# A decoder trunk's head in a new order, and the attention's two heads normalised on one engine

## The chip, the cores and the metric

The kernel runs on one core of a Trainium2 chip. The core has a matrix engine (TensorE, PE in the profile; its weight loads are listed as PEld), VectorE (DVE), ScalarE (ACT), GpSimd (POOL) and SyncE (SP), which here issues nearly all DMAs. Each engine takes its own instructions in their order; between engines they are ordered by semaphores. SBUF is the on-chip memory, PSUM the banks that PE accumulates in.

The metric is device time in microseconds (us) of one execution, as the median of several timed runs. A profiled execution is one more run, with a trace; its span reaches from the program's first instruction to its last.

## The reference

One layer of a decoder trunk, in float32, for a sequence of 2048 rows and a width of 1024:

```python
mod = jax.nn.silu(c) @ w_ada[l] + b_ada[l]
shift, scale, gate = jnp.split(mod, 3, axis=-1)
u = x * (1.0 + scale[:, None, :]) + shift[:, None, :]
h = u @ w_in[l]
q, k, v, a_gate, p_in, p_gate, m_a, m_p = jnp.split(h, offsets, axis=-1)
a = sliding_window_sink_attention(q, k, v, sinks[l], bias, mask) * jax.nn.silu(a_gate)
a = a @ w_attn_proj[l]
p = jnp.einsum('bsgc,gcd->bsgd', multiscale_causal_pool(p_in), w_pool_mix[l]).reshape(B, S, POOL_WIDTH)
p = (p * pool_scale[l]) * jax.nn.silu(p_gate)
p = p @ w_pool_proj[l]
y = jax.nn.sigmoid(m_a) * a + jax.nn.sigmoid(m_p) * p
y = (y @ w_out[l]) * (1.0 + gate[:, None, :])
x = layer_norm(DEEPNORM_ALPHA * x + y, ln_gain[l], ln_bias[l])
```

The attention has 16 query heads of 64 on 2 key heads, a window of 128 keys, a relative bias and one sink a head in the softmax. Before all of this, `mod` has to be known: a product of a 1024 vector with a 1024 x 3072 matrix.

## The kernel before

**Products.** The large products are made by a 2 x 2 block scheme with seven block products instead of eight. The activations of a chunk (two halves of 512 columns, eight tiles of 128 rows) are kept as seven sets in SBUF, `B11, T1, T2, B21, T3, B22, T4`: the blocks and their differences. A set has four tiles, and each tile a high and a low half in a reduced float format; a float32 product is three matmuls (`mm3`: high x high, high x low, low x high). Making a tile is a cast on ACT (the high half) and a subtraction on DVE (the low half): `parts`, `split_set`. The weights go the same way: a `Quad` (line 235) is a pair of 128 x 1024 weight tiles, loaded by `load_w` and `load_last`; `mid` (258) and `late` (268) are the differences of its blocks, and `split_part` (418) or `pair_split` makes high and low halves of two at a time (`w_set`). A quad's four stages are F (`B11, T1`), S (`T2, B21`), Th (`T3, B22`) and L (`T4`). It accumulates in three PSUM banks `a, b, c`; `behind` (451) evacuates and adds between the products, and `consume` takes each finished block.

**The order.** `plan` lists all products of all phases; `run` (477) walks through them. At a product's position it makes the weights' halves that are due, then issues the twelve matmuls, then `behind`, then `tick` (330): it runs the functions hung on that position (`at`, `hooks`) and those put off by `defer(ticks, f)` (313). So the place of a call in this walk is its place in the engine's queue, SP's too.

**The head** (`head`, 1212) comes before the walk. It computes `mod` tile by tile (k = 0 to 7), turns `x` into `u`, fills the first sets and makes the first group's products of stages F and S by itself, written out by hand. The group is two quads, `grp[0]` (keys and values) and `grp[1]` (queries 0 and 1). For each k: `opening(k)` is 16 one-column matmuls for `shift` (`pe_modulation`, 1256) and on DVE a multiply-reduce over 1024 columns for `scale` and an addition that waits for PE (`modulation`, 1263). `difference(k)` (1292, k < 4) subtracts the halves of `x`; `closing(k)` (1297) makes a tile of T1 from it (k < 4) or of T2 (k >= 4); `modulate_x(k)` applies scale and shift on ACT; `middle(k)` (1285) makes the tile of B11 (k < 4) or B21, and for k >= 4 first updates `ts[k - 4]`, from which T2 is made. `products(i)` (1312) issues tile i of B11 and T1 for both quads, `more(x, i)` (1339) tile i of T2 and B21 for quad x, six matmuls. `second_pair(x)` (1330) makes the weights of stage S and copies the accumulators `a` and `b` to a bank and a buffer, on ACT. `t3_sum(i)` (1307) makes the blocks of T3. `idle_products` are matmuls on a constant tile whose result is not used.

In the loop at line 1357, `closing` comes one or two turns after its `difference`, and the sets T3 and the third weights come after the last product. The head then returns four functions that the walk runs at its positions 0, 3, 4 and 5 (`late` of the second quad, the sets B22 and T4). The walk finds F and S of the first group done (`opened`) and begins with their `behind`.

Beside the first group run `fold_parts` (1108), which multiplies the pooling weights with the mixing matrix, and `gate_modulation`; both load through SP.

**The overlay** (`overlay`, 767) is the attention. Its 64 steps a chunk (two heads each) are spread between the matmuls of the phases `o0` and `o1`. `step(n)` (871) issues on PE: scores of n into the bank `lg`, transposes of n-2 into the bank `pt`, values of n-3 into `pv`. Both `lg` and `pt` are single banks. Then, for n-1, DVE takes the reciprocal of the softmax sums and the two heads are scaled: the first by ACT, the second by DVE's `tensor_scalar`. Then ACT casts `pt` to `pth` and copies a part of `pv`; for n, DVE reads `lg` for each head (a custom operation that adds the bias and takes the minimum) and ACT takes exponentials; then DVE subtracts `ptl` from `pt` and `pth`, which frees `pt`, and adds the outputs.

**Stores of q.** `q_quad` (574) scales a finished block on ACT, splits it on DVE and stores both halves two ticks later, from a ring of buffers `c`.

Of the kernel before, what the change touches and what calls it, by code (L numbers as in the profile page):

```python
# [59 lines left out]
def kernel(  # L60
# [174 lines left out]
    class Quad:  # L235
        def __init__(self, srcs, consume, sums=None, again=False):
            self.srcs, self.consume, self.sums, self.again = srcs, consume, sums, again
            self.at, self.parts, self.rings, self.opened, self.prefetch = {}, {}, {}, False, None

# [211 lines left out]
    def behind(ph, q, kind, h):  # L451
# [11 lines left out]
        elif kind == "S":  # L463
            if h == 0:
                dve.tensor_tensor(q.b, q.c, q.p5, ALU.add)
            else:
                q.consume(ph, 0, 0, q.a)
        elif kind == "Th":
            if h == 0:
                dve.tensor_tensor(q.p5, q.c, q.p5, ALU.add)  # L470
                q.consume(ph, 1, 1, q.p5)
            else:
                q.consume(ph, 0, 1, q.b)
        else:
            q.consume(ph, 1, 0, q.c)
# [98 lines left out]
    def q_quad(s, m):  # L574
        def consume(ph, mi, t, src):
            hi, lo = ph.c("q_hi", F32R), ph.c("q_lo", F32R)
            act.activation(hi, src, AF.Copy, scale=-0.125)
            dve.scalar_tensor_tensor(lo, src, -0.125, as32(hi), ALU.mult, ALU.subtract)
            defer(2, lambda: [sp.dma_start(q_d[s, m + mi, t, n], as32(x)) for n, x in enumerate((hi, lo))])
# [187 lines left out]
    def overlay(ph, s, n_slots):  # L767
# [103 lines left out]
        def step(n):  # L871
# [4 lines left out]
            if n - 1 in Es:  # L876
                E, e0, sm = Es.pop(n - 1)
                dve.reciprocal(sm, sm)
                act.activation(E[:, 0, e0:256], E[:, 0, e0:256], AF.Copy, scale=sm[:, 0:1])
                dve.tensor_scalar(E[:, 1, e0:256], E[:, 1, e0:256], sm[:, 1:2], None, ALU.mult)  # L880
# [331 lines left out]
    def head(ph, grp):  # L1212
# [50 lines left out]
        def modulation(k):  # L1263
            m = KT + k
            w = ws[k][1]
            dve.tensor_tensor_reduce(w, w, cb, 1.0, mod[:, m : m + 1], ALU.mult, ALU.add, mod[:, m : m + 1])
            dve.tensor_tensor(mod[:, k : k + 1], mod[:, k : k + 1], sums[k][:, 0:1], ALU.add)
# [13 lines left out]
        def opening(k):  # L1281
            pe_modulation(k)
            modulation(k)
# [63 lines left out]
        difference(0)  # L1347
        modulate_x(0)
# [3 lines left out]
        difference(1)  # L1352
        middle(0)
        closing(0)
        modulate_x(1)
        first_pair(1)
        for k in range(2, KT):
            if k == 6:
                second_pair(0)
                closing(4)  # L1360
            opening(k)
            if k < 4:
                difference(k)
            if 2 < k < 6:
                closing(k - 2)
            middle(k - 1)
            if k == 7:
                closing(5)
            modulate_x(k)
            if k < 6:  # L1370
                products(k - 2)
            if k < 4:
                grp[k - 2].mid(dve)
            if k == 6:
                more(0, 0)
                second_pair(1)
        more(1, 0)
        for x in range(2):
            more(x, 1)
        closing(6)  # L1380
        middle(7)
        closing(7)
        for i in range(2):
            t3_sum(i)
        for i in (2, 3):
            for x in range(2):
                more(x, i)
        grp[0].late(dve)
        for i in (2, 3):
            t3_sum(i)  # L1390
        sets["T3"] = set_tile("T3")
        for i in range(4):
            parts("T3", i, xs[i][0])
# [3 lines left out]
        grp[0].parts["Th"] = third  # L1397

# [10 lines left out]
        rest = (0, lambda: grp[1].late(dve)), (3, late_parts("B22", 1)), (4, t4_sums), (5, late_parts("T4", 0))  # L1409
        for q, o in zip(grp, opened):  # L1410
            q.a, q.b, q.c, _, q.p5 = o
            q.opened = True
        return rest
# [153 lines left out]
```

## Time and profile before

| | us |
|---|---|
| timed runs, median of 3 (lowest, highest) | 1715.49 (1715.05, 1715.85) |
| profiled execution, its own time | 1721.38 |
| its span | 1719.3 |
| mean granted clock of PE | 0.989 |
| busy: PE | 1672.1 |
| busy: DVE | 1274.5 |
| busy: ACT | 945.4 |
| busy: POOL | 590.5 |

Stretches of the profiled execution, in us from the span's start: the head up to about 65, the first phase of the walk to about 167, the overlays from about 168 to 490 and from 750 to 1075.

A row of a timeline reads: start, duration, engine, line, operation, what it writes `<-` what it reads by the program's names, shapes, how many in a row; in brackets the idle time of the engine before it and what ended it. The line is 56 for nearly all, that of a helper that records every operation, so rows are told apart by their names. A row "SPq" is a DMA being issued. A row of a chain of waits has start, duration, what.

### The profile page before, as it was taken

Reading aid. Unit: us, or ns where it says so; the run is one execution under the profiler, and the core shown is the slowest. Engines: PE = TensorE matmul, PEld = TensorE weight load, DVE = VectorE, ACT = ScalarE, POOL = GpSimd, SP = SyncE. Lnnn points to the kernel's source line nnn. Section 1 sums busy time; section 2 is a strip of 40 time slices with the busy share of each in tenths; the row PEclk is TensorE's granted clock in tenths of the full one; section 3 lists DMA queues with packets and bytes.
Section 4 is the critical chain, followed back from the end, with each engine's and each line's share of the span. In section 5 each row is a group of like instructions: output and inputs, shape, how many; then the busy total and the mean of one; then the engine's idle time right before and its main releaser. Section 6 shows DMA issues by size and latency. Waiting matters only on the chain.

```text
span 1719.3 us, 24847 instructions
## 1 busy us (share of the span) xinstructions
PE 1672.1 (97%) x8112; PEld 1400.3 (81%) x8112; DVE 1274.5 (74%) x2295; ACT 945.4 (55%) x1815; POOL 590.5 (34%) x563
## 2 busy tenths in 40 slices
PE   9899999989999999999999999999999999999997
PEld 7678788878788888888888888888878888888886
DVE  5956787778756778658877888487886785778778
ACT  3644687767753436447777676433454443434552
POOL 3012455545553223323334243322243311113544
PEclk8999999999999999999999999999999999999999
DMA  9389666766547789873555544489978695778343
GB/s 355 120 285 301 204 213 228 244 214 201 190 162 228 254 281 316 285 249 119 183 178 188 180 145 154 160 268 325 336 260 290 199 331 182 259 261 295 147 147 122
DMA packets 236545, 389.50 MB, mean 227 GB/s; under 512 B 20840, under 2 KB 90240, under 8 KB 236288
## 3 DMA queue, kind: packets, MB, share of 16 engines
q1 hardware_dynamic: 235344, 386.55, 66.9%
q10 hardware_dynamic: 1040, 1.34, 0.3%
q8 instruction: 64, 1.05, 0.3%
q14 instruction: 65, 0.53, 0.1%
q0 software_dynamic: 32, 0.02, 0.0%
HBM read 243.63 MB, written 147.35 MB: 227 GB/s over the span
## 4 chain that ended last, share of the span: by engine, by line
PE 74%; DVE 10%; DMA 6%; ACT 5%; issue 4%; SPq 1%; POOL 0%; DVEq 0%; ACTq 0%; POOLq 0%
PE mm L56 46%; PE lg L56 12%; PE c L56 10%; PE pv L56 3%; PE pt L56 3%; DVE w_set L56 3%; DVE L L56 2%; ACT L L56 2%; ACT w_set L56 1%; DVE wide L56 1%; SPq L56 1%; DMA A<-in_win_dram 1%; ACT sig L56 1%; DMA qs<-q_d 1%; ACT q_hi L56 1%
## 5 line engine op out<-in xcount | busy, mean ns | idle before, releaser
L56 PE MATMUL mm<-set_B,w_set 128*128 128x512 f32 x2664 | 655.6, 393 | 1.5 <-DVE w_set L56 1.3
L56 PEld LDWEIGHTS mm<-set_B,w_set 128*128 128x128 f32 x2664 | 498.5, 189 | 105.5 <-DVE w_set L56 2.2
L56 PE MATMUL mm<-set_T,w_set 128*128 128x512 f32 x1896 | 470.4, 395 | 1.7 <-DVE set_T L56 0.9
L56 POOL TENSOR_TENSOR W<-W 128x512 f32<-128x512 f32 x185 | 267.2, 1454 | 568.3 <-DVE w_set L56 373.7
L56 PEld LDWEIGHTS mm<-set_T,w_set 128*128 128x128 f32 x1896 | 354.9, 191 | 75.4 <-DVE set_T L56 1.6
L56 DVE TENSOR_TENSOR w_set<-W,w_set 128x1024 fp32r<-128x1024 f32 x197 | 254.7, 1293 | 111.9 <-ACT w_set L56 101.9
L56 ACT CAST w_set<-W 128x1024 fp32r<-128x1024 f32 x222 | 232.2, 1047 | 92.8 <-PE mm L56 52.9
L56 ACT ACTIVATE L<-L 128x257 f32<-128x257 f32 (+3 forms) x384 | 191.2, 500 | 117.8 <-DVE L L56 117.2
L56 PE MATMUL lg<-set_T,w_set 128*128 128x512 f32 x828 | 201.1, 390 | 4.4 <-DVE set_T L56 2.3
L56 PE MATMUL c<-set_T,w_set 128*128 128x512 f32 x828 | 199.8, 390 | 0.0
L56 PEld LDWEIGHTS lg<-set_T,w_set 128*128 128x128 f32 x828 | 155.0, 188 | 37.9 <-DVE set_T L56 3.5
L56 PEld LDWEIGHTS c<-set_T,w_set 128*128 128x128 f32 x828 | 155.0, 188 | 32.1
L56 POOL TENSOR_TENSOR W<-W,A 128x512 f32<-128x512 f32 x41 | 56.2, 1371 | 283.6 <-DMA A<-in_win_dram 135.8
L56 DVE CUSTOM_DVE_ANT_0 L<-lg,bt,nsink 128x256 f32<-128x256 f32 (+1 forms) x256 | 111.0, 470 | 23.8 <-PE lg L56 17.5
L56 DVE TENSOR_TENSOR ptl<-pt,pth 128x512 fp32r<-128x512 f32 (+1 forms) x128 | 85.8, 670 | 30.3 <-ACT pth L56 29.3
L56 PEld LDWEIGHTS lg<-kk,qs 128*128 128x128 f32 x512 | 76.5, 189 | 36.7 <-DVE L L56 26.3
L56 PE MATMUL lg<-kk,qs 128*128 128x256 f32 (+1 forms) x512 | 83.6, 286 | 18.2 <-DVE L L56 17.6
L56 DVE TENSOR_SCALAR L<-L 128x256 f32<-128x256 f32 (+1 forms) x128 | 96.9, 757 | 4.5
L56 ACT ACTIVATE sig<-mm 128x512 f32<-128x512 f32 x76 | 45.5, 599 | 96.9 <-PE mm L56 94.7
L56 ACT CAST pth<-pt 128x512 fp32r<-128x512 f32 (+1 forms) x128 | 72.4, 565 | 24.6 <-PE pv L56 23.9
L56 POOL TENSOR_TENSOR w_set<-W,w_set 128x1024 fp32r<-128x1024 f32 x25 | 61.3, 2452 | 56.8 <-ACT w_set L56 31.1
L56 PE MATMUL pv<-pth,vv 128*128 128x256 f32 x248 | 75.4, 325 | 1.9 <-DMA vv<-v_d 1.9
(208 smaller groups left out, 1957.4 us busy)
## 6 DMA issues: line engine op xcount, KB each, us to landing
W<-in_win_dram SPq DMA_DIRECT2D x40, 512.0 KB, 5.8
qs<-q_d SPq DMA_DIRECT2D x128, 128.0 KB, 4.6
sums_d<-W SPq DMA_DIRECT2D x62, 256.0 KB, 4.2
W<-sums_d SPq DMA_DIRECT2D x31, 512.0 KB, 3.6
ain_d<-st SPq DMA_DIRECT2D x56, 256.0 KB, 3.6
A<-in_win_dram SPq DMA_DIRECT2D x42, 256.0 KB, 5.8
q_d<-q_hi SPq DMA_DIRECT2D x32, 256.0 KB, 3.9
q_d<-q_lo SPq DMA_DIRECT2D x32, 256.0 KB, 4.0
```

The lines of the kernel that those rows point to most:

```text
L56: return lambda *args, **kw: self.tc.keep_in_program_order(op(*args, **kw))
```

## The change

Five edits. (1) In `step`, both heads of n-1 are scaled by ACT. (2) `q_quad` with m = 0 (the quad of the first group of each chunk) stores after one tick instead of two. (3) The head's order: `closing(k)` for T1 follows its `difference(k)`; the two `mid` move into `opening(4)` and `opening(5)`, between DVE's reduction and the addition that waits for PE; the modulation of k = 6 precedes `products(3)`; both `second_pair` follow each other; T3's blocks, casts and low halves are spread over `opening(6)`, `opening(7)` and the last products. (4) The tiles 2 and 3 of T2 and B21 are multiplied quad by quad instead of tile by tile. (5) The sum `q.b = q.c + q.p5` of each of the two quads is made at the head's end instead of in the walk (`summed`).

```diff
@@ -236,6 +236,7 @@
         def __init__(self, srcs, consume, sums=None, again=False):
             self.srcs, self.consume, self.sums, self.again = srcs, consume, sums, again
             self.at, self.parts, self.rings, self.opened, self.prefetch = {}, {}, {}, False, None
+            self.summed = False
 
         def load_w(self, ph, q=sp, a12=True):
             self.w = x = ph.weights()
@@ -462,7 +463,8 @@
                 act.copy(q.p5, q.b)
         elif kind == "S":
             if h == 0:
-                dve.tensor_tensor(q.b, q.c, q.p5, ALU.add)
+                if not q.summed:
+                    dve.tensor_tensor(q.b, q.c, q.p5, ALU.add)
             else:
                 q.consume(ph, 0, 0, q.a)
         elif kind == "Th":
@@ -576,7 +578,7 @@
             hi, lo = ph.c("q_hi", F32R), ph.c("q_lo", F32R)
             act.activation(hi, src, AF.Copy, scale=-0.125)
             dve.scalar_tensor_tensor(lo, src, -0.125, as32(hi), ALU.mult, ALU.subtract)
-            defer(2, lambda: [sp.dma_start(q_d[s, m + mi, t, n], as32(x)) for n, x in enumerate((hi, lo))])
+            defer(2 if m else 1, lambda: [sp.dma_start(q_d[s, m + mi, t, n], as32(x)) for n, x in enumerate((hi, lo))])
 
         kept = (sums_d[1 + m // 2], s == 1) if m else ()
         return Quad((win[TQ + m], win[TQ + m + 1]), consume, *kept)
@@ -876,8 +878,8 @@
             if n - 1 in Es:
                 E, e0, sm = Es.pop(n - 1)
                 dve.reciprocal(sm, sm)
-                act.activation(E[:, 0, e0:256], E[:, 0, e0:256], AF.Copy, scale=sm[:, 0:1])
-                dve.tensor_scalar(E[:, 1, e0:256], E[:, 1, e0:256], sm[:, 1:2], None, ALU.mult)
+                for h in range(2):
+                    act.activation(E[:, h, e0:256], E[:, h, e0:256], AF.Copy, scale=sm[:, h : h + 1])
             if pt is not None:
                 h0 = k0_of(n - 2) // P
                 hi = tp.tile([P, 2, 2, P], F32R, tag="pth", bufs=1, name="pth")
@@ -1260,10 +1262,11 @@
             for i in range(KT):
                 mm(sums[k][:, 0:1], ws[k][0][:, i * P : (i + 1) * P], ct[:, i : i + 1], start=i == 0, stop=i == KT - 1)
 
-        def modulation(k):
+        def modulation(k, fill):
             m = KT + k
             w = ws[k][1]
             dve.tensor_tensor_reduce(w, w, cb, 1.0, mod[:, m : m + 1], ALU.mult, ALU.add, mod[:, m : m + 1])
+            fill()
             dve.tensor_tensor(mod[:, k : k + 1], mod[:, k : k + 1], sums[k][:, 0:1], ALU.add)
 
         def modulate_x(k):
@@ -1278,9 +1281,9 @@
         def parts(name, i, src):
             split_set(name, i, src, (act, dve))
 
-        def opening(k):
+        def opening(k, fill=lambda: None):
             pe_modulation(k)
-            modulation(k)
+            modulation(k, fill)
 
         def middle(k):
 
@@ -1345,56 +1348,78 @@
         opening(0)
         idle_products(18)
         difference(0)
+        closing(0)
         modulate_x(0)
         first_pair(0)
         opening(1)
         idle_products(14)
         difference(1)
+        closing(1)
         middle(0)
-        closing(0)
         modulate_x(1)
         first_pair(1)
-        for k in range(2, KT):
-            if k == 6:
-                second_pair(0)
-                closing(4)
-            opening(k)
+        for k in range(2, 5):
+            opening(k, (lambda: grp[0].mid(dve)) if k == 4 else lambda: None)
             if k < 4:
                 difference(k)
-            if 2 < k < 6:
-                closing(k - 2)
+                closing(k)
             middle(k - 1)
-            if k == 7:
-                closing(5)
             modulate_x(k)
-            if k < 6:
-                products(k - 2)
-            if k < 4:
-                grp[k - 2].mid(dve)
-            if k == 6:
-                more(0, 0)
-                second_pair(1)
+            products(k - 2)
+        sets["T3"] = set_tile("T3")
+
+        def third_sums(*ks):
+            return lambda: [t3_sum(i) for i in ks]
+
+        def third_casts(*ks):
+            for i in ks:
+                act.copy(sets["T3"][:, i, 0, :], xs[i][0])
+
+        def third_lows(*ks):
+            t = sets["T3"]
+            return lambda: [low(dve, t[:, i, 1, :], xs[i][0], t[:, i, 0, :]) for i in ks]
+
+        opening(5, lambda: grp[1].mid(dve))
+        middle(4)
+        closing(4)
+        modulate_x(5)
+        opening(6, third_sums(0))
+        products(3)
+        middle(5)
+        closing(5)
+        second_pair(0)
+        second_pair(1)
+        modulate_x(6)
+        third_casts(0)
+        opening(7, third_sums(1))
+        third_lows(0)()
+        more(0, 0)
         more(1, 0)
-        for x in range(2):
-            more(x, 1)
+        middle(6)
         closing(6)
+        modulate_x(7)
+        more(0, 1)
+        more(1, 1)
         middle(7)
         closing(7)
-        for i in range(2):
-            t3_sum(i)
-        for i in (2, 3):
-            for x in range(2):
+        third_casts(1)
+        third_sums(2, 3)()
+        third_lows(1)()
+        third_casts(2, 3)
+        third_lows(2, 3)()
+        for x in range(2):
+            for i in (2, 3):
                 more(x, i)
         grp[0].late(dve)
-        for i in (2, 3):
-            t3_sum(i)
-        sets["T3"] = set_tile("T3")
-        for i in range(4):
-            parts("T3", i, xs[i][0])
+        for q, o in zip(grp, opened):
+            q.a, q.b, q.c, _, q.p5 = o
+            q.opened = q.summed = True
+        dve.tensor_tensor(grp[0].b, grp[0].c, grp[0].p5, ALU.add)
         third = [ph.split(False) for _ in range(2)]
         act.copy(by_two(third[0]), grp[0].third())
         low(dve, by_two(third[1]), grp[0].third(), by_two(third[0]))
         grp[0].parts["Th"] = third
+        dve.tensor_tensor(grp[1].b, grp[1].c, grp[1].p5, ALU.add)
 
         def t4_sums():
             for i in range(4):
@@ -1406,11 +1431,7 @@
 
         sets["B22"] = set_tile("B22")
         dve.tensor_scalar(nsink, nsink, -1.0, None, ALU.mult)
-        rest = (0, lambda: grp[1].late(dve)), (3, late_parts("B22", 1)), (4, t4_sums), (5, late_parts("T4", 0))
-        for q, o in zip(grp, opened):
-            q.a, q.b, q.c, _, q.p5 = o
-            q.opened = True
-        return rest
+        return (0, lambda: grp[1].late(dve)), (3, late_parts("B22", 1)), (4, t4_sums), (5, late_parts("T4", 0))
 
     def first_start(ph, phase):
         rest = head(ph, phase["groups"][0])
```

## The prediction

> **What bounds the kernel now.** I read the page first, then what TensorE (PE) waited for in the whole span, then the stretches of the head.
>
> ```profile
> span 1719.3 us, 24847 instructions
> PE 1672.1 (97%) x8112; PEld 1400.3 (81%) x8112; DVE 1274.5 (74%) x2295; ACT 945.4 (55%) x1815; POOL 590.5 (34%) x563
> ```
>
> PE is busy for 97% of the span, so an edit on VectorE (DVE) or ScalarE (ACT) is worth only what it takes out of PE's gaps, or out of stretches where PE is busy with fillers or at a low clock.
>
> ```profile
> PE lg L56 <- DVE L L56: 17.6, 17, 3.3
> PE pv L56 <- ACT st L56: 3.8, 1, 3.8
> ```
>
> The columns are us in total, times, longest. The first row is the attention overlay of `step(n)`: the scores' one bank `lg` is not yet read by DVE when PE wants to write it, 17 times. The second is the largest of the head, which has another loss, in the granted clock (the column before the last two):
>
> ```profile
> 27.82:41.48 13.66, 13.00 (x41) 11.07 (x42) 6.25 (x11) 4.74 (x9) 0.00 (x0) 0.50 1.04 404
> 42.90:79.90 37.00, 29.70 (x135) 23.14 (x134) 33.87 (x55) 24.67 (x40) 2.21 (x1) 0.95 0.28 87
> 80.00:98.40 18.40, 14.12 (x83) 12.42 (x83) 9.98 (x15) 8.30 (x15) 3.85 (x3) 1.00 0.97 322
> ```
>
> Columns: stretch, length, busy us of PE, PE's weight loads, DVE, ACT, POOL, clock, DMA share, GB/s. Until 41.5 us the head is bound by its loads (404 GB/s, DMA full) with PE at half clock; from 42.9 to 79.9 by DVE (33.9 of 37.0 us); from 80 to 98.4 by the DMA queues. After that PE is full until the overlay.
>
> **Part 1: ACT normalises both heads (`step`).** In each of 128 steps one DVE `tensor_scalar` goes and one ACT `activation` comes.
>
> ```profile
> L56 DVE TENSOR_SCALAR L<-L x128: 289/357/2317, 173.6 to 1073.2; 128x256 f32<-128x256 f32 x120, 128x128 f32<-128x128 f32 x8
> ```
>
> Median 0.36 us, but up to 2.3. One stalled step shows why that matters:
>
> ```profile
> 467.79 0.15 DVE L56 RECIPROCAL L<-L 128x2 f32<-128x2 f32 x1
> 467.95 1.26 POOL L56 TENSOR_TENSOR W<-W 128x512 f32<-128x512 f32 x1 [1.16 <-DVE L L56]
> 467.98 1.39 DVE L56 TENSOR_SCALAR L<-L 128x256 f32<-128x256 f32 x1
> 468.04 0.51 ACT L56 ACTIVATE L<-L 128x256 f32<-128x256 f32 x1 [2.35 <-DVE L L56]
> 468.45 0.57 ACT L56 CAST pth<-pt 128x512 fp32r<-128x512 f32 x1
> ...
> 469.28 0.47 DVE L56 CUSTOM_DVE_ANT_0 L<-lg,bt,nsink 128x256 f32<-128x256 f32 x1
> ...
> 470.09 0.68 DVE L56 TENSOR_TENSOR ptl<-pt,pth 128x512 fp32r<-128x512 f32 x1
> ...
> 470.23 0.74 PE L56 MATMUL lg<-kk,qs 128*128 128x256 f32 x4 [2.14 <-DVE L L56]
> ...
> 470.83 0.66 PE L56 MATMUL pt<-ident,L 128*128 128x128 f32 x4
> ```
>
> POOL's subtraction starts 0.03 us before the `tensor_scalar`, which then lasts until POOL ends: 1.39 us instead of 0.36. Only then are the two reads of `lg` made. Without it they start 1.3 us earlier (469.28 - 467.98), and PE could write `lg` at 468.9. But the transposes that follow write `pt`, which is free only after `ptl`; `ptl` needs `pth` from ACT; and in ACT's order the new activation stands before `pth` and puts it off by 0.41 (468.45 - 468.04). So `pth` ends at 469.43, `ptl` at about 470.2, the transposes start at 470.24 instead of 470.83. **The stall shrinks by 0.6, not by 1.3; its rest moves from `lg` to `pt`.** Of the seventeen stalls, the first and the last here,
>
> ```profile
> 181.28 1.12 PE L56 MATMUL lg<-kk,qs 128*128 128x256 f32 x4 [1.85 <-DVE L L56]
> ...
> 1053.05 0.74 PE L56 MATMUL lg<-kk,qs 128*128 128x256 f32 x4 [1.74 <-DVE L L56]
> ```
>
> seven are shorter than 0.6 (0.43, 0.28, 0.36, 0.26, 0.35, 0.51, 0.32) and go whole: 2.5. Ten give 0.6 each: 6.0; the first, with half the `pth` to cast, some 0.5 more. Together 9.0.
>
> Where no stall is, `tensor_scalar` is short and the change costs:
>
> ```profile
> 792.96 0.36 DVE L56 TENSOR_SCALAR L<-L 128x256 f32<-128x256 f32 x1
> ...
> 794.17 0.69 DVE L56 TENSOR_TENSOR ptl<-pt,pth 128x512 fp32r<-128x512 f32 x1
> ...
> 795.14 0.60 PE L56 MATMUL pt<-ident,L 128*128 128x128 f32 x4
> ```
>
> Here `ptl` is already bound by ACT's `pth`; 0.41 later plus the wait's own 0.03 makes 0.44. Its end (794.86) lies 0.28 before the transposes, so PE would now wait some 0.2. Going through all steps this way, nine lose something (0.29, 0.07, 0.12, 0.22, 0.35, 0.21, 0.06, 0.07, 0.07), 1.5 together. Net of part 1: **-7.5** (bounds: 0, and -14.5 if nothing but the `lg` reads counted, the seven short ones whole and ten at up to 1.3 or 1.4).
>
> The rule for that upper bound is in the Trainium skill, SBUF — State Buffer, section Who interferes with whom: VectorE and GpSimd share one port pair as an exclusive lock, `tensor_scalar` can take it, ScalarE waits for nobody. The trace agrees (1.39 beside POOL, 0.36 without).
>
> ACT gets 128 x 0.41 = 52 us more, beside PE. Its cover is its idle time:
>
> ```profile
> 160.00:500.00 340.00, 327.37 (x1747) 278.18 (x1746) 253.76 (x662) 244.12 (x584) 164.32 (x180) 0.98 0.66 212
> 740.00:1080.00 340.00, 332.45 (x1814) 284.15 (x1813) 262.21 (x668) 241.51 (x573) 119.11 (x131) 1.00 0.53 170
> ```
>
> ACT stands at 244 of 340; plus 64 x 0.41 = 26 it is 270, or 79%. What queues behind the new activation on ACT is `pth`, the copy `o`, two exponentials and the weights' casts, all 0.41 later; for `pth` that is counted above, for the casts nothing, since in these stretches no wait of PE on `w_set` shows.
>
> **Part 2: the clock after those stalls.** Three of the long stalls are followed by a stretch at half clock:
>
> ```profile
> 181.42:184.84 3.42, 3.42 (x14) 3.13 (x15) 2.18 (x9) 2.82 (x10) 1.14 (x2) 0.50 0.44 132
> 382.80:386.22 3.42, 3.42 (x11) 2.74 (x10) 2.54 (x10) 3.37 (x10) 1.43 (x2) 0.50 0.77 234
> 471.55:474.97 3.42, 3.42 (x11) 2.75 (x10) 2.84 (x10) 2.50 (x7) 0.19 (x1) 0.50 0.83 255
> 178.00:181.40 3.40, 1.54 (x8) 0.94 (x7) 3.36 (x8) 1.26 (x4) 2.41 (x4) 1.00 0.77 283
> 379.40:382.80 3.40, 1.22 (x9) 1.15 (x10) 3.35 (x9) 2.80 (x8) 2.64 (x4) 1.00 1.08 409
> 468.10:471.50 3.40, 1.27 (x10) 1.21 (x11) 3.15 (x8) 2.92 (x9) 2.53 (x3) 1.00 0.08 29
> ```
>
> Each costs 1.7 (PE is busy for all 3.42 at 0.50), and the 3.4 us before it held 1.2 to 1.5 us of PE work. With 0.6 to 1.1 more they hold 1.8 to 2.6. I take two of three as avoided: **-3.4** (bounds 0 and -5.1).
>
> A rule speaks against this term: the Trainium skill, TensorE: Matmul & The Clock Gate, section Why this matters for your kernels, has the clock fall after an idle gap of about 3 us. Here it fell after gaps of 1.85 and 2.14, so the trace disagrees; by the rule alone this term is nothing.
>
> **Part 3: the head.** No operation is saved here; all is order. The two gaps into which work moves are these, DVE waiting in its order for PE's modulation at half clock:
>
> ```profile
> 35.50 0.16 DVE L56 TENSOR_TENSOR mod<-mod,pv 128x1 f32<-128x1 f32 x1 [4.06 <-PE pv L56]
> 42.90 0.15 DVE L56 TENSOR_TENSOR mod<-mod,pt 128x1 f32<-128x1 f32 x1 [4.76 <-PE pt L56]
> ```
>
> I walked the new order engine by engine, with the durations of the old head (DVE 0.6 for 512 columns, 1.28 for the reduction, 1.2 for 1024; ACT 0.5 a copy or cast, 0.75 a modulation, 1.0 a cast of 1024; twelve matmuls 2.8, or 5.9 at half clock) and the clock stepping each 3.4 us as recorded. `difference` and `closing` now follow each other with an ACT operation between, so DVE waits 0.75 in four turns; this takes what the two `mid` (1.29 each) give by moving into the two gaps.
>
> PE: `products(1)` begins at 27.1, with B11's second tile, and ends at 31.5, since the clock still halves at 27.8; the modulation of k = 4 ends at 33.4, `products(2)` at 37.9, k = 5 at 39.9, k = 6 at 42.1, now ahead of `products(3)`, which ends at 46.4. ACT then sets the pace: after the bank is cleared (46.8) four copies and a double cast to 49.8, k = 6 modulated at 51.3, casts of T3 and B21 to 52.3, of T2 (behind DVE's sum and low half) at 53.9, k = 7 modulated at 55.4, B21's cast 55.9, T2's last 56.8. DVE: T2's last low half 57.4; two sums and three low halves of T3 60.4; `late` and the first quad's sum 61.6; the third weights, cast by 62.1, low half 63.4; the second quad's sum, `late`, the low halves of k and q, 65.9; four of `B22` 68.3. Before:
>
> ```profile
> 45.04 0.85 PE L56 MATMUL mm<-set_T,w_set 128*128 128x512 f32 x3
> ...
> 58.90 0.69 DVE L56 TENSOR_TENSOR set_T<-head_T,set_T 128x512 fp32r<-128x512 f32 x1
> ...
> 64.93 1.22 DVE L56 TENSOR_TENSOR w_set<-W,w_set 128x1024 fp32r<-128x1024 f32 x1
> ...
> 70.34 1.29 DVE L56 TENSOR_TENSOR set_B<-head_small,set_B 128x512 fp32r<-128x512 f32 x2
> ```
>
> So `products(3)` ends 0.5 later than its 45.9, T2 2.2 earlier than 59.6, the third weights 2.7 earlier than 66.1, `B22` 3.3 earlier than 71.6, for four operations of T3 and the quads' two sums no longer stand between. **-3.3.** With the clock full throughout, the same walk ends 6.7 early; with `products(3)` at half clock to its end (48.0), 1.6 less than that, 1.7. Quad by quad, the first quad's accumulation ends 2.8 (two tiles of six matmuls) before the second's instead of 1.4, so that its sum is made while PE works on the second.
>
> The DMA-bound stretch after 80 is issued by the same program positions, so it should move along. In it `q_quad(s, 0)` stores a tick earlier: SP's order then has the first pair before the load that blocks SP's queue from 70.23,
>
> ```profile
> 70.23 6.71 SPq L56 DMA_DIRECT2D room_raw<-in_wpt_dram  x2
> 76.98 0.60 SPq L56 DMA_DIRECT2D q_d<-q_hi  x1
> ...
> 97.79 0.59 ACT L56 COPY st<-pv 128x512 f32<-128x512 f32 x1 [1.34 <-DMA wmix_d<-st]
> 98.43 0.65 PE pv L56 x4
> ```
>
> so 0.5 MB leaves the burst: at 322 GB/s at most 1.6. But the wait of PE ends with `st`, whose slot is freed by a later store. **-0.8** (0 to -1.6).
>
> **Sum.** 7.5 + 3.4 + 3.3 + 0.8 = 15.0 us. The profiled execution took 1721.38 (span 1719.3 and 2.1 around it), 5.9 above the median of the timed runs, 1715.49; taken from the median: **1700.5**.
>
> **Rivals.**
> - The dips stay, since the stretches ahead of them remain short of PE work: 15.0 - 3.4 = 11.6, so 1704. For: the stall at 381 still is 2.6 of its 3.26. 0.14. The Trainium skill's rule on the clock gives this time too, for another reason.
> - The head gives nothing: what it wins is waited for again in the DMA stretch (share 0.97), and one dip of the three stays: 15.0 - 3.3 - 0.8 - 1.7 = 9.2, so 1706. Against: 0.28 DMA share from 42.9 to 79.9 leaves room. 0.18.
> - `pt` does not hold PE, all dips go, and the head keeps its clock: 14.5 + 5.1 + 6.7 + 1.6 = 28, so 1687.5. Against: the order of `pth` and `ptl` in the step at 468. 0.11.
> - The change moves nothing measurable, since the waits only change their name: within 3.4 of 1715.5. 0.06.
> - Slower: the 0.44 on `ptl` in the half of the steps with a short `tensor_scalar` (its median is 0.36), if their slack at the transposes is below 0.44: 64 x 0.44 = 28, less the 9.0 and the head's 4.1: 15 slower, 1730. It decides where ACT arrives late at `pth`. Against: only nine steps have so little slack. 0.07.
>
> **Chances and range.** The forecast has 0.44. Faster by over 0.2% (3.4 us, about what a measurement of this kernel can tell from no change) is the forecast and the first three rivals, 0.44 + 0.14 + 0.18 + 0.11 = 0.87; same 0.06; slower 0.07. The range 1690 to 1709 takes in the forecast, the first two rivals, and both ends of parts 1 and 3 where they do not coincide.
>
> **What would show it.** Part 1: no `tensor_scalar` on L, 256 activations on ACT, PE's wait for `DVE L` below 8 us, a new wait of `pt` on `ptl` of some 5 to 8. Part 2: fewer half-clock stretches between 181 and 475. Part 3: B22's last tile near 68, PE's gap before 98 some 4 earlier. Wrong if PE's waits on ACT or on `w_set` appear in the overlay, or if the head's clock takes another course.

## The result, and the profile after

| | before | after |
|---|---|---|
| timed runs, median of 20 each, us (lowest, highest) | 1716.28 (1713.15, 1723.97) | 1711.19 (1705.64, 1714.39) |
| ratio to before (95% interval) | | 0.9962 (0.9951 to 0.9972) |
| profiled execution, its own time (span), us | 1721.38 (1719.3) | 1713.51 (1711.7) |

By the ratio the change is faster by 0.38%, some 6.5 us (4.8 to 8.4), where 15.0 were forecast; 1711.19 lies above the forecast range. (The ratio and its interval are the record's estimate from the timed runs; the quotient of the two medians is 0.9970.) From the page of the changed kernel:

```profile
span 1711.7 us, 24940 instructions
PE 1668.9 (98%) x8112; PEld 1398.8 (82%) x8112; DVE 1181.5 (69%) x2167; ACT 987.5 (58%) x1943; POOL 589.6 (34%) x563
```

DVE lost 128 instructions and 93 us, ACT got 128 and 42 us, and the span shrank by 7.6: the engines' sums do not give the time. What PE waited for says more (us in total, times, longest):

```profile
PE pt L56 <- DVE ptl L56: 8.1, 16, 0.7
PE pv L56 <- ACT st L56: 4.2, 1, 4.2
PE lg L56 <- DVE L L56: 3.2, 4, 1.0
PE pv L56 <- DMA vv<-v_d: 2.7, 1, 2.7
...
PE pt L56 <- ACT L L56: 1.2, 3, 0.7
```

The wait for `DVE L` fell from 17.6 to 3.2, and a wait that was not there, `pt` for `ptl`, is 8.1 us in 16 steps. Three transposes wait for the scaled heads themselves, now ACT's (the last row). The wait of the head for `st` is no shorter than before (4.2 against 3.8).

The step that the prediction took as its example, in a timeline of the changed kernel:

```profile
464.49 0.46 DVE L56 CUSTOM_DVE_ANT_0 L<-lg,bt,nsink 128x256 f32<-128x256 f32 x1
464.57 1.28 POOL L56 TENSOR_TENSOR W<-W 128x512 f32<-128x512 f32 x1 [1.16 <-DVE L L56]
464.66 0.91 ACT L56 ACTIVATE L<-L 128x256 f32<-128x256 f32 x2 [2.06 <-DVE L L56]
...
465.42 0.74 PE L56 MATMUL lg<-kk,qs 128*128 128x256 f32 x4 [0.93 <-DVE L L56]
465.48 0.57 ACT L56 CAST pth<-pt 128x512 fp32r<-128x512 f32 x1
...
466.07 0.69 DVE L56 TENSOR_TENSOR ptl<-pt,pth 128x512 fp32r<-128x512 f32 x1 [0.71 <-ACT pth L56]
...
466.82 0.66 PE L56 MATMUL pt<-ident,L 128*128 128x128 f32 x4 [0.67 <-DVE ptl L56]
```

DVE's read of `lg` follows the reciprocal at once, beside POOL's subtraction, and lasts 0.46; PE's wait at `lg` is 0.93 instead of 2.14. But the two activations take ACT until 465.57, `pth` ends at 466.05, `ptl` at 466.76, and PE waits another 0.67 for `pt`. The step won 2.14 - 0.93 - 0.67 = 0.54; the prediction said 0.6. The scaling no longer waits for POOL: the two activations take 0.91 here, beside POOL's subtraction, and 0.91 in the next step (469.43), where POOL does nothing. The Trainium skill, SBUF — State Buffer, section Who interferes with whom, has ScalarE waiting for no other engine's port; the trace agrees, by these two figures.

All overlay steps together, the gaps of PE before `lg`, `pt` and `pv`: before 18.2, 0 and 2.0 (sum 20.2), after 3.2, 9.6 and 2.7 (15.5). The seventeen waits for DVE's reads gained 7.9, after what PE now waits at `lg` and `pt` in the same steps, and three small gaps at `lg` 0.6; nine other steps now wait at `pt`, 3.0 together (six of them 0.68, 0.67, 0.49, 0.42, 0.41 and 0.18); the one wait for a load of `vv` grew by 0.7.

Where the rest went shows when the same operations of DVE and ACT are paired between the two traces; the median shift in each stretch, after against before:

| stretch of the span, us | shift, us |
|---|---|
| 72 to 80 | -2.1 |
| 98 to 170 | -0.14 |
| 190 to 225, behind the stall at 181 | -2.9 |
| 240 to 300 | -2.1 |
| 350 to 370 | -0.5 |
| 390 to 420, behind the stall at 381 | -3.7 |
| 500 to 700, behind the first overlay | -4.1 |
| from 1080, behind the second | -7.0 |
| end | -7.6 |

In this pair of profiles the head's 2.1 us are gone at 98, and the overlays brought the whole gain. Within the first overlay it goes to and fro: most of what the stall at 181 gives is lost again by 350, in the new waits at `pt` and the longer one for `vv`. The chain at 98, first of the profile before, then of the changed one (SPq is a DMA's issue on SP):

```profile
92.42 0.52 SPq L56 DMA_DIRECT2D wmix_d<-st  x1
...
94.55 0.48 SPq L56 DMA_DIRECT2D q_d<-q_hi  x1
95.21 0.32 SPq L56 DMA_DIRECT2D q_d<-q_lo  x1
```

```profile
91.12 0.93 SPq L56 DMA_DIRECT2D q_d<-q_hi  x1
92.09 0.76 SPq L56 DMA_DIRECT2D q_d<-q_lo  x1
92.90 0.63 SPq L56 DMA_DIRECT2D wmix_d<-st  x1
...
97.65 0.59 ACT L56 COPY st<-pv 128x512 f32<-128x512 f32 x1 [4.40 <-DMA wmix_d<-st]
...
98.29 0.70 PE L56 MATMUL pv<-ident,vt 128*128 128x128 f32 x4 [4.25 <-ACT st L56]
```

With the stores of q a tick earlier, their third pair stands ahead of the store `wmix_d<-st` in SP's order instead of behind it. That store frees the slot that ACT's copy `st` waits for; it is issued 0.5 later than before, although PE's work ahead of it (the first fold, below) ran 2.1 earlier, and `st` and PE start at 97.65 and 98.29, as before (97.79 and 98.43). So the earlier stores were my first suspect for the lost head, and the head's clock the second.

### The profile page after: what moved, and what is told of

It reads as the page before. It is cut to its first block, busy times and chain, and to the rows that moved or that the text cites. A ratio compares the mean times of both kernels' runs of the same rounds, so it can differ in the third digit from the quotient of the medians.

```text
span 1711.7 us, 24940 instructions
## 1 busy us (share of the span) xinstructions
PE 1668.9 (98%) x8112; PEld 1398.8 (82%) x8112; DVE 1181.5 (69%) x2167; ACT 987.5 (58%) x1943; POOL 589.6 (34%) x563
## 4 chain that ended last, share of the span: by engine, by line
PE 64%; ACT 7%; DVE 5%; DMA 4%; issue 3%; POOL 1%; SPq 0%; DVEq 0%; ACTq 0%; POOLq 0%
PE mm L56 40%; PE lg L56 11%; PE c L56 9%; ACT L L56 3%; PE pv L56 2%; PE pt L56 2%; DVE w_set L56 1%; ACT pth L56 1%; ACT w_set L56 1%; DVE wide L56 1%; DMA W<-in_wap_dram 1%; DMA vv<-v_d 1%; ACT sig L56 1%; DVE ptl L56 1%; DMA e_rep<-e_d 0%
## 5 line engine op out<-in xcount | busy, mean ns | idle before, releaser
L56 ACT ACTIVATE L<-L 128x257 f32<-128x257 f32 (+3 forms) x512 | 241.3, 498 | 97.0 <-DVE L L56 96.4
L56 PE MATMUL pt<-ident,L 128*128 128x128 f32 x496 | 76.6, 276 | 9.6 <-DVE ptl L56 8.1
```

What stands on the lines that cost most here:

```text
L56: return lambda *args, **kw: self.tc.keep_in_program_order(op(*args, **kw))
```

## The experiments

Before was timed anew beside each group of runs (medians 1714.91, 1714.70 and 1714.40 us), and a difference in us below is the ratio's, on that median. "Stretch" is the time from the start of the eleven folded products of `fold_parts` (78.48 in the changed kernel) to the transposes that end the wait at 98; it is 17.9 before and 19.8 after. "First fold" is the start of the product ahead of these.

**Parts one by one.** e1: before with edit (1), the scaling on ACT, alone.

```diff
-                act.activation(E[:, 0, e0:256], E[:, 0, e0:256], AF.Copy, scale=sm[:, 0:1])
-                dve.tensor_scalar(E[:, 1, e0:256], E[:, 1, e0:256], sm[:, 1:2], None, ALU.mult)
+                for h in range(2):
+                    act.activation(E[:, h, e0:256], E[:, h, e0:256], AF.Copy, scale=sm[:, h : h + 1])
```

> The kernel before with the first edit alone: ACT scales both heads, DVE's tensor_scalar on L is gone. Theory (the stall moves from lg to pt): PE's waits in the overlay go from 18.2 us on lg to about 3 on lg and 9 to 10 on pt, 5 to 6 less in sum; with one or two half-clock stretches less (1.7 each) the time falls by 6 to 9 us, that is all that the whole change won. Rival (the gain came from the head or from its other timing): less than 3 us, and lg waits above 10 us.

e2: edits (3) to (5), the head, alone: the changed kernel with these two places as before.

```diff
-            defer(2 if m else 1, lambda: [sp.dma_start(q_d[s, m + mi, t, n], as32(x)) for n, x in enumerate((hi, lo))])
+            defer(2, lambda: [sp.dma_start(q_d[s, m + mi, t, n], as32(x)) for n, x in enumerate((hi, lo))])
...
-                for h in range(2):
-                    act.activation(E[:, h, e0:256], E[:, h, e0:256], AF.Copy, scale=sm[:, h : h + 1])
+                act.activation(E[:, 0, e0:256], E[:, 0, e0:256], AF.Copy, scale=sm[:, 0:1])
+                dve.tensor_scalar(E[:, 1, e0:256], E[:, 1, e0:256], sm[:, 1:2], None, ALU.mult)
```

> The kernel before with the head's new order and the two early sums alone, no earlier store of q and DVE's tensor_scalar kept. Theory (the earlier store gave the head's gain back): everything is 2.1 us earlier near 75 us and stays so past the wait before 98, whose length stays near 3.8 us; time 2 us lower. Rival (the DMA queues bound the stretch of 80 to 98 whatever is ahead of it): the wait before 98 grows to 5 to 6 us and from 100 us on nothing is earlier; time unchanged.

e3: edit (2), the stores a tick earlier, alone in the kernel before (`defer(2 if m else 1, ...)`). e4: the changed kernel without it (`defer(2, ...)`).

> The kernel before with the second edit alone: the quad of q in the first group stores one tick earlier. Theory: the third pair's two stores now stand ahead of the pooling weights' store that frees the slot of st; PE's wait before 98 grows from 3.8 to about 5.5 us and all that follows is 1.5 to 2 us later; time 2 us higher. Rival (the order of stores does not matter, the queue's total does): wait near 3.8 or shorter, time unchanged.

> The changed kernel with the second edit undone (stores of q after two ticks everywhere). Theory: PE's wait before 98 falls from 4.25 to about 2.2 to 3.8 us, the walk is about 2 us earlier than in the changed kernel from 100 us on, time 2 us below it. Rival: the wait stays above 4 us and the time is that of the changed kernel.

| | median, us | ratio (95%) | PE's gaps before lg, pt | stretch | wait before the transposes |
|---|---|---|---|---|---|
| e1, scaling on ACT alone | 1708.32 | 0.9966 (0.9954 to 0.9978) | 3.3, 10.1 | 18.0 | 3.9 |
| e2, head alone | 1713.61 | 0.9994 (0.9983 to 1.0006) | 18.5, 0 | 17.8 | 2.1 |
| e3, earlier stores alone | 1717.14 | 1.0020 (1.0008 to 1.0031) | 18.6, 0 | 20.0 | 4.4 |
| e4, change without earlier stores | 1707.04 | 0.9960 (0.9947 to 0.9974) | 3.1, 9.7 | 17.9 | 3.8 |

The scaling on ACT alone has the whole gain of the change (0.9966 against 0.9962), with the same trade of waits:

```profile
PE pt L56 <- DVE ptl L56: 8.8, 17, 0.7
...
PE lg L56 <- DVE L L56: 3.1, 4, 1.0
```

The head alone is worth -1.0 us, with an interval from -2.9 to +1.0 that holds no change. In e2's profile the new head's gain is not waited for again: the wait before the transposes is 2.1, not the 5 to 6 of its rival (nor the 3.8 of the theory). The earlier stores make the stretch 2 us longer and, alone, the kernel slower by 0.2% (3.4 us, 1.4 to 5.3), just measurably; the wait grew to 4.4, not to 5.5. Inside the change their cost isn't told apart from nothing (0.9960 without, 0.9962 with), where e4 was expected 2 us below the changed kernel. The stretch also depends on the clock: e8 below, with the order of stores of before, has 19.0, and PE was at half clock from 75.6 to 82.5 in its profile. That the stores alone are enough shows in e11 below, the changed kernel with a full clock in that stretch: 20.1.

**The clock of the head.** e1 and before have the same head, to the instruction. Their stretches at the place where before runs at half clock (length, busy us of PE, PE's loads, DVE, ACT, POOL, clock, DMA share, GB/s), before first:

```profile
24.41:27.82 3.41, 3.20 (x23) 2.58 (x21) 3.27 (x8) 1.53 (x5) 0.00 (x0) 1.00 1.03 401
27.82:41.47 13.65, 12.99 (x41) 11.06 (x42) 6.25 (x11) 4.74 (x9) 0.00 (x0) 0.50 1.04 404
```

```profile
24.00:27.41 3.41, 3.41 (x25) 3.11 (x24) 2.98 (x6) 2.03 (x4) 0.00 (x0) 1.00 1.02 399
27.41:41.06 13.65, 12.38 (x68) 10.00 (x68) 10.16 (x20) 7.23 (x12) 0.00 (x0) 1.00 1.04 401
```

The same head ran at half clock for 13.65 us in one execution and at full clock in the other, and PE did 68 matmuls in place of 41. So I tabulated every profile's head: half-clock time from 17 us to the first fold, and that fold's start. (Ahead of 17 us all but before, e7 and e11 had 3.4 us of half clock more, e9 6.8.)

| head | half clock, us -> first fold, us |
|---|---|
| old | before 17.1 -> 78.56; e7 13.7 -> 78.48; e3 6.8 -> 73.29; e8 6.8 -> 74.53; e1 3.4 -> 73.91 |
| new | after 10.2 -> 76.46; e9 10.2 -> 76.45; e11 10.2 -> 75.70; e6 10.2 -> 75.89; e4 6.8 -> 74.77; e2 3.4 -> 73.18; e5 3.4 -> 73.21 |

At 3.4 us of half clock the new order is 0.7 earlier; at 6.8 it lies 0.2 and 1.5 behind the two draws of the old one. The means are 75.8 (five draws) and 75.1 (seven). The profile from which I predicted had the longest half-clock time of these twelve.

**The new wait.** If `pt` waits because `pth` stands behind two activations on ACT, putting `pth` ahead of them should take it away. e5 is e4 with the block of `Es.pop(n - 1)` moved behind the cast:

```diff
-            if n - 1 in Es:
-                E, e0, sm = Es.pop(n - 1)
-                dve.reciprocal(sm, sm)
-                for h in range(2):
-                    act.activation(E[:, h, e0:256], E[:, h, e0:256], AF.Copy, scale=sm[:, h : h + 1])
             if pt is not None:
...
+            if n - 1 in Es:
+                E, e0, sm = Es.pop(n - 1)
+                dve.reciprocal(sm, sm)
+                for h in range(2):
+                    act.activation(E[:, h, e0:256], E[:, h, e0:256], AF.Copy, scale=sm[:, h : h + 1])
```

> The changed kernel with the stores of q after two ticks, and in step(n) the cast of pt to pth ahead of the two activations that scale E. Theory (the wait moved to pt because the added activation puts pth off): pth is cast while ACT waits for the reciprocal, ptl follows the two reads of lg at once, and PE's waits in the overlay fall from 12.8 us (3 on lg, 10 on pt) to 5 or less; time 8 to 10 us below the kernel with only the stores undone, near 1698. Rival (ACT has become the bound of these steps): waits stay above 9 us, on pt or on L, and the time is within 3 us of that kernel.

1690.82 us, ratio 0.9867 (0.9851 to 0.9884). One step of it, and its overlays' two windows beside the changed kernel's:

```profile
458.62 0.59 ACT L56 CAST pth<-pt 128x512 fp32r<-128x512 f32 x1
...
459.10 0.92 ACT L56 ACTIVATE L<-L 128x256 f32<-128x256 f32 x2
...
459.25 0.69 DVE L56 TENSOR_TENSOR ptl<-pt,pth 128x512 fp32r<-128x512 f32 x1 [1.09 <-ACT pth L56]
...
461.26 0.64 PE L56 MATMUL lg<-kk,qs 128*128 128x256 f32 x4
...
461.73 0.60 PE L56 MATMUL pt<-ident,L 128*128 128x128 f32 x4
```

```profile
165.00:500.00 335.00, 330.66 (x1794) 282.62 (x1793) 215.33 (x632) 270.89 (x654) 174.16 (x189) 1.00 0.66 219
735.00:1080.00 345.00, 344.78 (x1883) 297.60 (x1882) 224.41 (x609) 270.56 (x645) 124.04 (x134) 1.00 0.53 174
```

```profile
165.00:500.00 335.00, 323.70 (x1744) 275.08 (x1743) 208.84 (x601) 264.80 (x648) 163.56 (x181) 0.99 0.66 213
735.00:1080.00 345.00, 340.21 (x1852) 291.74 (x1851) 220.54 (x609) 265.82 (x642) 123.44 (x136) 1.00 0.52 170
```

`ptl` starts beside the activations, over a microsecond before PE wants `pt`; no wait of `pt` for `ptl` is left in the list, and the gaps before `lg` are 3.6. PE's idle time in the two windows is 4.3 + 0.2 = 4.6 us against 11.3 + 4.8 = 16.1 in the changed kernel, and the first window runs at full clock. The time fell by 16 us against e4, where I had expected 8 to 10; PE's idle time in the windows explains 10.7 of it, from 15.2 in e4. Against before (20.2 us idle in these windows, and 6.8 us lost in four half-clock stretches) the account is 15.6 + 6.8 = 22.4. The two profiled executions differ by 31.0, of which 5.5 had been won by 98, with the head's clock; so the account leaves 3 of the other 25.5 open. That it also comes close to the ratio's 22.8 (19.9 to 25.5) is in part luck, since the profile of before had a lower mean clock (0.989) than most runs of before (median 0.991).

Is it the order alone? e7 is before with the same block behind the cast, but with the second head still scaled by DVE. e8 is before with only the `tensor_scalar` moved behind `ptl`:

```diff
-                dve.tensor_scalar(E[:, 1, e0:256], E[:, 1, e0:256], sm[:, 1:2], None, ALU.mult)
+                second = E[:, 1, e0:256], sm[:, 1:2]
...
+            if second:
+                dve.tensor_scalar(second[0], second[0], second[1], None, ALU.mult)
```

> The kernel before, with the cast of pt to pth ahead of the reciprocal and the two scalings, which stay one on ACT and one on DVE. Theory: DVE's tensor_scalar still stands ahead of the reads of lg, and is held by POOL for up to 1.4 us, so the waits on lg stay near 18 us and the time is that of the kernel before within 2 us. Rival (the order of pth alone makes the gain): waits below 12 us.

> The kernel before, with DVE's tensor_scalar on the second head kept on DVE but issued behind the reads of lg and behind ptl. Theory (what counts is what stands ahead of the reads of lg and of ptl, not which engine scales): waits on lg fall below 3 us and on pt stay below 3, since pth is not put off; time 10 us below the kernel before or more. Rival (DVE's load in these phases is the bound, so only moving work to ACT helps): waits above 10 us in sum.

e7: 1715.45, ratio 1.0003 (0.9994 to 1.0012); PE's gaps are 14.9 before `lg`, less than the 18 that I expected, and 0.3 before `pt`, and yet no gain in the time. e8: 1700.04, 0.9908 (0.9895 to 0.9922); in its list of waits

```profile
PE pt L56 <- DVE L L56: 4.3, 7, 0.9
...
PE lg L56 <- DVE L L56: 2.1, 3, 1.0
```

the two reads of `lg` are free of the `tensor_scalar`, `pth` is not put off, and what is left is the transposes' wait for the scaled head itself (4.3, where I had expected under 3). So both halves are needed: `tensor_scalar` out of the way of the `lg` reads, and nothing new ahead of `pth` on ACT. e7 has the second alone and gains nothing, e1 the first alone and gains 0.34%, e8 both, in the head of before, and gains 0.92%, e5 both and gains 1.33%, with the new head's 1.0 us in it. So it is not the load of DVE that counts: e8 leaves the scaling there.

**The wait before 98.** e6 is e5 with the folded weights stored at once; e9 is e6 with the earlier stores of q back.

```diff
-            defer(1, lambda: sp.dma_start(dst, st))
+            sp.dma_start(dst, st)
```

> As the kernel before in this list, and the folded pooling weights are stored from st at once instead of one tick later, so ahead of the other stores in SP's queue. Theory (the stretch of 80 to 98 is set by the store that frees the slot of st): PE's wait before 98 falls from 3.8 us to below 1.5, and all after it is 2 to 4 us earlier. Rival (the DMA queues are full there, and another transfer ends the wait): the wait stays above 3 us.

> The kernel with pth first and the folded weights stored at once, and the stores of q one tick earlier again (the second edit of the change put back). Theory (two rings of buffers are late before 98: st until the folded weights have landed, q_hi until an earlier q has; each edit alone only pulls the one and pushes the other): now both land early and PE's wait before 98 falls from 2.0 to 2.4 us to below 1; the stretch from the first folded product to that wait's end, 17.7 to 18.0 us in the kernels without the second edit and 19.8 to 20.0 with it, falls to 16.5 or less; time 1 to 2 us lower. Rival (the transfers of that stretch as a whole set its length): 17.7 us or more as before, time unchanged.

e6: 1690.26, 0.9854 (0.9839 to 0.9869). The wait stayed, 2.4 us where I had expected under 1.5, with another end:

```profile
94.77 0.60 ACT L56 ACTIVATE q_hi<-c 128x512 fp32r<-128x512 f32 x1 [4.89 <-DMA q_d<-q_hi]
95.26 0.58 ACT L56 COPY st<-pv 128x512 f32<-128x512 f32 x1
95.89 0.66 PE L56 MATMUL pv<-ident,vt 128*128 128x128 f32 x4 [2.38 <-ACT st L56]
```

`st` follows `q_hi` on ACT, and `q_hi` waits for a slot of the ring `c` that a store of q frees. `st` needs both stores early. With both (e9) it waits for neither:

```profile
92.46 0.60 ACT L56 ACTIVATE q_hi<-c 128x512 fp32r<-128x512 f32 x1 [2.25 <-PE c L56]
92.95 0.58 ACT L56 COPY st<-pv 128x512 f32<-128x512 f32 x1
93.69 0.60 PE L56 MATMUL pv<-ident,vt 128*128 128x128 f32 x4
```

The stretch is 15.2 (e10 below, with the same stores, has 15.5), where e5 has 17.7, e6 18.0 and before 17.9. The time, 1689.93, 0.9859 (0.9845 to 0.9874), cannot be told from e5's and e6's, where 1 to 2 us less were expected: the some 2.5 us of the stretch are within the intervals, and this profile's head drew 10.2 us of half clock where e5's drew 3.4.

**A try on the clock.** e10 is e9 with the one-column matmuls of `pe_modulation` issued between the products of `products(k - 2)`, so that less one-column work stands together (that of k = 5 and 7 still does).

```diff
-        def pe_modulation(k):
+        def pe_modulation(k, between=()):
...
+                if i % 2 and between:
+                    between[i // 2]()
...
-            products(k - 2)
```

> As e9, and in the head the one-column matmuls of the modulation of k = 2 to 4 and 6 are issued between the matmuls of products(k - 2) and products(3), two and then three at a time, instead of ahead of them. Theory (the head's length depends on how the clock's windows of 3.4 us fall on stretches of one-column matmuls): no half-clock stretch between 15 and 45 us, the first folded product at 75 us or earlier. Rival (DVE and ACT set the head's pace and the clock does not matter, or the additions behind the modulations come later and cost what the clock gives): first folded product at 76 us or later.

It failed: 1698.51, 0.9909 (0.9894 to 0.9925), over 8 us slower than e9, with the first fold at 85.84. The stretch up to the clock's fall, and the one at half clock:

```profile
24.10:27.53 3.43, 2.29 (x14) 1.72 (x12) 2.58 (x6) 1.93 (x4) 0.00 (x0) 1.00 1.04 404
27.53:65.10 37.57, 37.25 (x124) 32.23 (x125) 21.96 (x38) 15.58 (x27) 0.00 (x0) 0.50 0.46 178
```

PE counts as busy for 37.25 of 37.57 us and stays at half clock all the while. So a full PE of the profile is not what brings the clock back. In before, too, the clock fell behind a step in which PE was busy for 3.20 of 3.41 us. PE's rows ahead of the return at 65.1:

```profile
57.83 2.70 PE L56 MATMUL pt<-ct,head_big 128*128 128x1 f32 x12
...
61.82 1.48 PE L56 MATMUL mm<-set_B,w_set 128*128 128x512 f32 x3
```

From 60.5 to the return no one-column matmul runs, and the 3.4 us ahead of 65.1 are the first since 27.5 without any. That one-column matmuls count for little with the clock would fit this; it was not tested, and at 41.5 in before the clock came back behind a step with five of them.

**Once more.** e11 is the changed kernel again, unchanged.

> The changed kernel once more, for another draw of where the clock's windows fall in the head. Theory: the stretch from the first folded product to the end of the wait before 98 is 19.8 us again (set by the order of stores), while the time of that first product moves with the clock's half stretches, between 75 and 79 us. Rival: the first product stays at 78.5 us and the stretch varies.

1709.58, 0.9973 (0.9962 to 0.9984); stretch 20.1 and a wait of 6.0 before the transposes, first fold 75.70. The time agrees with the first measurement, and the long stretch is found again.

## Why the prediction was right in direction and wrong in size

The sum, term by term:

| term | forecast, us | measured, us |
|---|---|---|
| part 1, PE's gaps | -7.5 | -4.7 (profiles before and after); -5.7 (e1's profile) |
| part 2, clock behind the stalls | -3.4 | two half-clock stretches fewer, as forecast |
| parts 1 and 2, as time | -10.9 | -5.8 (-3.8 to -7.9), e1 |
| part 3, the head | -3.3 | -1.0 (-2.9 to +1.0), e2 |
| stores a tick earlier | -0.8 | +3.4 (+1.4 to +5.3), e3; inside the change not told from nothing |
| sum | -15.0 | -6.5 (-4.8 to -8.4) |

The single runs do not add up to the whole (-3.4 against -6.5), since e3's loss is not found inside the change. Two terms fail in their mechanism and lie outside what was measured, the head's walk and the stores; parts 1 and 2 have the mechanism right and are too large, and carry most of the 8.5 us that are missing.

- **Part 1, -7.5: mechanism right, size too large.** In the example step the stall shrank by 0.54 where 0.6 was worked out, its rest moved from `lg` to `pt`, and the wait of `pt` for `ptl`, forecast at 5 to 8, was 8.1 (all gaps before `pt` 9.6, with 1.2 of waits for ACT's `L`; the prediction had named waits on ACT as a sign of being wrong). The seventeen stalls, 9.0 by the forecast, gave 7.9. The price of `pth` put off, "nine lose something ... 1.5 together", was 3.0, in nine steps: the mis-sized term. A wait for `vv` took 0.7 back, and three small gaps gave 0.6. That `pth` behind the activations is the cause, e5 shows: with it ahead of them the waits of `pt` are gone.
- **Part 2, -3.4: as forecast in the profiles, not separately shown in the time.** The half-clock stretches at 181 and 382 are gone. The one at 471 stayed, 4 us earlier:

```profile
464.00:467.41 3.41, 1.82 (x12) 1.19 (x11) 2.53 (x9) 2.72 (x8) 2.63 (x3) 1.00 0.21 77
467.41:470.82 3.41, 3.41 (x12) 2.83 (x11) 1.56 (x6) 2.48 (x6) 0.19 (x1) 0.50 0.58 154
```

  With 1.82 us of PE work ahead, where before had 1.27, the clock still fell; the forecast took 1.8 to 2.6 as enough for two of three. All traces together bear the term out: between 165 and 1080 us the kernels with the `tensor_scalar` ahead of the reads of `lg` have 4 (before), 3 (e2), 3 (e3) and 2 (e7) half-clock stretches of 3.4 us, those with the scaling on ACT 2 (changed), 1 (e11), 1 (e4) and none (e1), and e8 has 1, and e5, e6, e9 and e10 none. Between the first two groups that is two fewer on the average. Parts 1 and 2 together, -10.9, were measured by e1 at -5.8 (-3.8 to -7.9); e2 against e4, the same edit with the new head, gives 5.8 too. The gaps (5.7 in e1's profile) alone would make that; with two stretches beside them it would be 9.1. Where the other 3 us went the runs do not show; it stays open.
- **Part 3, -3.3: this step failed.** "I walked the new order ... and the clock stepping each 3.4 us as recorded" took one execution's clock for a property of the order; the clock took another course, which the prediction had named as a sign of being wrong. `B22` ended at 69.53, 2.1 earlier than before, where 68.3 was forecast; but the old head in e1 ended it at 66.97, earlier than the new one here. First the changed kernel's row, then e1's:

```profile
68.24 1.29 DVE L56 TENSOR_TENSOR set_B<-head_small,set_B 128x512 fp32r<-128x512 f32 x2
```

```profile
65.69 1.28 DVE L56 TENSOR_TENSOR set_B<-head_small,set_B 128x512 fp32r<-128x512 f32 x2
```

  e2, the new head with e1's 3.4 us of half clock, ended it at 66.24, 0.7 earlier than e1. By e2's time the order is worth -1.0 (-2.9 to +1.0), and -3.3 lies outside. Whether the walk is right under before's own clock stays open: no run of this new order drew 13.7 us or more of half clock behind 17 us. The bounds of the term, 1.7 to 6.7, did not hold zero.
- **Stores a tick earlier, -0.8: wrong sign.** I moved 0.5 MB out of the burst and named the slot that "a later store" frees, but didn't follow the stores of q past that store in SP's order. They passed it: in e3 the stretch grew by 2.1 and the time by 0.2%.
- **Rivals.** Nearest was "The head gives nothing: what it wins is waited for again in the DMA stretch": the first profile looks like it (-2.1 before 80, -0.14 after 98). But e2 and e4 keep at the transposes what they had won at the first fold (5.4 and 3.8 us against before, then 5.5 and 3.8), so it is the order of stores and not the full queue that took it; and its 9.2 us were still more than the 6.5 measured, since it kept part 1 at full size. "`pt` does not hold PE" (28 us, 1687.5) is not what this change does. e5, without that wait, gains 22.8, near to it, but with other terms: the head gave 1.0 where that rival had 6.7, and the earlier stores, 1.6 there, are undone. The rival of a slower kernel fell with its premise: nine steps were short of slack, not half of them.

The best versions are e5, e6 and e9, at 1690 to 1691 us 1.4% below before and about 1% below the change.

## What to carry to other kernels

When work moves to an engine that isn't busy, look at what is queued behind it there: 0.41 us on ACT, at 58% load, kept back some two thirds of the gain (6.9 us in e4, 22.8 in e5) until one cast was put ahead of it. Before a stretch with a changing clock is optimised, profile it more than once; here the spread between executions of one order (73.3 to 78.6) was larger than the whole difference between two orders. A store that frees a buffer has a place in its queue's order: other stores moved past it put off everything that waits for the buffer.

## What the runs showed of the hardware

The granted clock of the same instructions differs from run to run: with the old head it was half for 3.4 to 17.1 us, counted from 17 us to the first fold. It changes at whole steps of about 3.41 us: in before at 27.82, 41.48, 48.30 and 51.72, which are 4, 2 and 1 such steps apart. In e1, the same head, it changed at 44.01 and 47.42, and counted back by five steps that is 26.9, where before has 27.82: the steps start elsewhere in each execution. So the same gap can lie within one step in one run and across two in another. The Trainium skill, TensorE: Matmul & The Clock Gate, section What's actually happening, has this window, running free of the kernel's start, and the difference between runs of one kernel; the traces agree. It puts the ramp's cost below 1% of a typical span; the spread here, 5.3 us at the first fold or 0.3%, lies within that, and is close to the 6.5 us that the change was worth.

That the clock can stay low for 37 us under a PE that the profile shows as 99% busy (e10, with one-column matmuls between the products) I had not expected, and the runs do not explain it.
